# The second adaLN block as TensorE products, the last expert's gate under the second projection ahead of it, its scatter sums in shared banks, query transposes later

## The chip, the cores and the metric

The kernel runs on one core of one Trainium2 chip. The metric is device time in microseconds (us) of one execution, launch to end. The median of three runs before the change is 1257.59 us (1257.53 to 1258.89).

## What is computed

One layer of a latent diffusion backbone, float32, with 256 tokens of width 1024. Cut to what matters here:

```python
sh1, sc1, g1, sh2, sc2, g2 = split(silu(c) @ ada_w + ada_b, 6)      # adaLN: a 1024 x 6144 product with one row
px = modulate(x, norm1_g, sh1, sc1) @ w_in + b_in                    # 5120 columns: q, k, v, hyena, gates
pc = modulate(ctx, norm1_g, sh1c, sc1c) @ w_in + b_in
# rope and qk-norm, differential attention over latent + context keys -> oa
# short convolution and FFT-like long convolution of the hyena columns -> ob
x = x + g1 * ((sigmoid(ga) * (oa @ w_up_a) + sigmoid(gb) * (ob @ w_up_b)) @ w_out)
# top-4-of-32 mixture of experts on modulate(x, norm2_g, sh2, sc2):
#   gate, up = split(h @ w1[e] + b1[e]); y = ((up+1) * gate * sigmoid(1.702 gate)) @ w2[e] + b2[e]
x = x + g2 * moe
```

`ada_w` has six column blocks of 1024. The kernel takes them two at a time: block 0 is sh1 and sc1, block 1 is g1 and sh2, block 2 is sc2 and g2.

## The kernel before

**Two stages.** In the front (from 0 to about 316 us) the adaLN products, the input projection, attention, the hyena branch, the merge and the router are computed. Then 32 experts follow: for each, the tokens chosen (at most 64) are gathered by a product, multiplied by `w1` (eight loads of 1 MB) and by `w2` (four loads of 1 MB), and scattered back by a product.

**What sets the order in the front.** The input projection is cut into pieces (q 0 to 3 and 8 to 11, h1 4 to 7 and 12 to 15, k 16 to 23, v 24 to 31, hv 32 to 39, h0 40 to 47, g0 48 to 55 and so on). The table `TASKS` names for each step of the other work the pieces after which its stages are issued; all engines' queues follow that order. A step `ada` also has its 1-MB load put into SyncE's queue at that place of the load order. All weights pass through 25 slots of 1 MB; the table `ROOM` says how many may hold loads, and `prefetch` issues the next load as soon as one is released, so a load's start is set by the release of an earlier one.

**The second adaLN block before.** `ada_step` (L628) adds up block 1 on VectorE: for each of eight k, two operations on 128x1024 (L639 for the first, L641 for the others) accumulate `col[:, k] * wt` into an SBUF array `AA1`. `ada1` (L981) then adds the 128 partitions up on TensorE: eight products with one column for sh2 (L659, which stand as 16 instructions in the trace) and two of 512 columns for g1 (L985).

**Other steps named below.** `q_out` transposes the rotated queries (`ps_qt`, L850), `k_out` the keys (`ps_kt`, L838, evicted to `KT` at L843 and L844), `v_rows` evicts the values (L974), `hyena` makes the convolved columns `HX` (L879, L880, L882) and `u_rows` transposes them (`ps_u`, L1107), `scores` reduces and exponentiates the attention scores (L1024, L1029). `ada_half` (L652) is the first adaLN block: 8 products per load, in four groups of 32 columns of the array, side by side in one PSUM bank.

**The end.** `up` (L1497) multiplies by `w1` as its loads land, `hidden` makes gate and up on VectorE and ScalarE (L1506 to L1511), `units` transposes the hidden units (L1517, copy L1519), `down` multiplies by `w2` (L1529), `down_last` does so for the last expert (L1586), `out_rows` multiplies by g2 (L1589), `scatter` (L1622) and `scatter_last` (L1593) put the rows back, L1595 adds them to the residual and L1596 writes the output. Under the last five `w1` loads, `last_but_one` scatters expert 30's rows (L1573) and adds them (L1574). Loads run on SyncE's queue (L332), eight outstanding.

## Time and profile before

| | |
|---|---|
| median of three runs | 1257.59 us |
| profiled execution | 1257.4 us |
| its span in the trace | 1255.7 us |
| TensorE busy | 1104.1 us (88%) |
| VectorE busy | 511.1 us (41%) |
| ScalarE busy | 276.7 us (22%) |
| GpSimd busy | 168.6 us (13%) |
| HBM read | 465.07 MB |
| mean granted TensorE clock | 0.982 |

A row of the timeline gives the start, the duration, the engine, the line, the operation with what it writes and reads, and in square brackets how long the engine had been idle before it and which engine, tile and line it was released by. A row of the windows gives for a stretch the busy time and instruction count of each engine, then the granted TensorE clock (1.00 is 2.4 GHz, 0.50 is 1.2 GHz), the share of time in which the DMA engines were busy, and GB/s. SPq is SyncE's queue: such a row is a load's issue, and its duration the time that the queue spent on it, waiting included.

### The profile page before, as it was taken

To read this page: it belongs to the slowest core of one execution; us is meant where nothing else is said; L and a number is where in the kernel's file an instruction comes from. 1 tells how busy PE (TensorE), PEld (TensorE's weight loads), DVE (VectorE), ACT (ScalarE), POOL (GpSimd) and SP (SyncE) were. 2 spreads that over 40 slices of the span, in tenths; PEclk is the share of its full clock that TensorE was granted. 3 is DMA by queue.
4 is the path that set the end of the run, shared out by engine and by line. 5 is a ranking of instruction groups with operands and counts; after the bars stand their busy time and mean duration, and the time that the engine had idled before them with its cause. 6 is when DMAs were issued, how large, how long until landed. Compare 5 with 4: busy or idle time off the path is not lost.

```text
span 1255.7 us, 14038 instructions
## 1 busy us (share of the span) xinstructions
PE 1104.1 (88%) x5547; PEld 532.6 (42%) x5547; DVE 511.1 (41%) x808; ACT 276.7 (22%) x503; POOL 168.6 (13%) x152
## 2 busy tenths in 40 slices
PE   7889789998999899897798879887988797888896
PEld 5678678897433433332242233223322332232222
DVE  5699996967222323331232223123212322223222
ACT  6563464654210111110010011001000100011110
POOL 2386455323000000000000000000000000000000
PEclk9999898999999999999999999999999999999998
DMA  9984534978899999999999999999999999999994
GB/s 335 400 313 148 175 134 191 347 293 358 334 412 417 417 417 417 418 417 418 417 416 417 417 417 417 417 417 417 418 418 418 417 417 418 417 418 417 417 416 177
DMA packets 98450, 467.10 MB, mean 372 GB/s; under 512 B 8800, under 2 KB 9804, under 8 KB 63564
## 3 DMA queue, kind: packets, MB, share of 16 engines
q1 hardware_dynamic: 95056, 462.26, 91.4%
q10 hardware_dynamic: 3324, 3.88, 1.0%
q8 instruction: 46, 0.75, 0.2%
q14 instruction: 24, 0.20, 0.0%
HBM read 465.07 MB, written 1.05 MB: 371 GB/s over the span
## 4 chain that ended last, share of the span: by engine, by line
DMA 54%; PE 28%; DVE 11%; ACT 2%; issue 2%; POOL 1%; ACTq 0%; SPq 0%; DVEq 0%; POOLq 0%
PE ps_eg L1497 6%; PE ps_eu L1497 6%; PE ps_ey L1529 5%; DMA w___w___10__3__4181<-in_exp_w_dram 2%; DMA w____w___18___0__5264<-in_exp_w_dram 2%; DMA w___w___28__7__6440<-in_exp_w_dram 2%; DMA w___w___20__3__5389<-in_exp_w_dram 2%; DMA w___w___11__7__4343<-in_exp_w_dram 2%; DMA w___w___22__3__5666<-in_exp_w_dram 2%; DMA w___w___14__3__4676<-in_exp_w_dram 2%; DMA w___w___24__3__5884<-in_exp_w_dram 2%; DMA w___w___18__3__5171<-in_exp_w_dram 2%; DMA w___w___26__3__6161<-in_exp_w_dram 2%; DMA w___w___27__7__6323<-in_exp_w_dram 2%; DMA w___w___23__7__5828<-in_exp_w_dram 2%
## 5 line engine op out<-in xcount | busy, mean ns | idle before, releaser
L1541 DVE TENSOR_TENSOR yr<-ps_ey,G 64x512 f32<-64x512 f32 x62 | 42.7, 688 | 387.2 <-PE ps_ey L1529 386.6
L479 POOL CAST pick<-both 128x128 fp32r<-128x128 f32 x32 | 24.6, 770 | 842.4 <-PE ps_eu L1380 842.3
L1542 ACT ACTIVATE YS<-yr,wsl 64x512 fp32r<-64x512 f32 x62 | 44.6, 719 | 402.9 <-DVE yr L1541 402.9
L1506 DVE TENSOR_SCALAR ga<-ps_eg 128x512 f32<-128x512 f32 x32 | 22.1, 691 | 163.4 <-PE ps_eg L1497 163.4
L1507 ACT ACTIVATE sg<-ga 128x512 f32<-128x512 f32 x32 | 20.2, 632 | 216.1 <-DVE ga L1506 216.1
L1543 DVE SCALAR_TENSOR_TENSOR YS<-yr,wsl,YS 64x512 fp32r<-64x512 f32 x62 | 46.3, 748 | 48.8 <-ACT YS L1542 48.8
L1452 PE MATMUL ps_xg<-S,XNh 128*128 128x256 f32 x128 | 37.6, 326 | 14.5 <-DVE S L1437 14.5
L1519 ACT COPY at<-ps_at 128x512 f32<-128x512 f32 x32 | 18.8, 586 | 142.6 <-PE ps_at L1517 142.6
L1627 DVE TENSOR_TENSOR X<-X,ps_sc 128x512 f32<-128x512 f32 x60 | 37.4, 680 | 3.0 <-PE ps_sc L1625 3.0
L397 PE MATMUL ps_g<-XTh,wsp 128*128 128x256 f32 x128 | 38.0, 297 | 0.0
L1452 PEld LDWEIGHTS ps_xg<-S,XNh 128*128 128x128 f32 x128 | 28.6, 223 | 19.6 <-DVE S L1437 16.9
L399 PE MATMUL ps_g<-XTh,wsp 128*128 128x256 f32 x128 | 36.5, 285 | 0.0
L398 PE MATMUL ps_g<-XTl,wsp 128*128 128x256 f32 x128 | 36.4, 285 | 0.0
L1452 PE MATMUL ps_xg<-S,XNl 128*128 128x256 f32 x128 | 36.1, 312 | 0.0
L1442 DVE TENSOR_SCALAR RAW<-ps_xg,s,sh 128x256 f32<-128x256 f32 x31 | 16.9, 544 | 35.3 <-ACT RAW L1444 35.3
L1622 PE MATMUL ps_sc<-YS,OT 128*128 128x512 f32 x120 | 30.9, 395 | 0.0
L1444 ACT ACTIVATE RAW<-ps_xg,sh,s 128x256 f32<-128x256 f32 x33 | 18.4, 564 | 49.2 <-PE ps_xg L1452 49.2
L1452 PEld LDWEIGHTS ps_xg<-S,XNl 128*128 128x128 f32 x128 | 28.7, 224 | 0.0
L397 PEld LDWEIGHTS ps_g<-XTh,wsp 128*128 128x128 f32 x128 | 24.6, 192 | 2.3 <-issue 1.8
L1622 PEld LDWEIGHTS ps_sc<-YS,OT 128*128 128x128 f32 x120 | 22.3, 188 | 7.2 <-issue 2.3
L399 PEld LDWEIGHTS ps_g<-XTh,wsp 128*128 128x128 f32 x128 | 24.7, 193 | 0.0
L398 PEld LDWEIGHTS ps_g<-XTl,wsp 128*128 128x128 f32 x128 | 24.6, 192 | 0.1
(1781 smaller groups left out, 2398.8 us busy)
## 6 DMA issues: line engine op xcount, KB each, us to landing
w_x<-in_x_dram SPq DMA_DIRECT2D x2, 512.0 KB, 4.9
w___ada___0__0__88<-in_ada_w_dram SPq DMA_DIRECT2D x2, 512.0 KB, 6.8
w___ada___0__1__91<-in_ada_w_dram SPq DMA_DIRECT2D x2, 512.0 KB, 9.5
w___ada___0__2__95<-in_ada_w_dram SPq DMA_DIRECT2D x2, 512.0 KB, 9.2
w___ada___0__3__98<-in_ada_w_dram SPq DMA_DIRECT2D x2, 512.0 KB, 12.1
...
w___in____h___0__104<-in_w_in_dram SPq DMA_DIRECT2D x1, 1024.0 KB, 12.8
w___ada___1__0__108<-in_ada_w_dram SPq DMA_DIRECT2D x2, 512.0 KB, 12.1
```

The costliest lines, as they stand in the source:

```text
L397: pe.matmul(ps, ahi, bhi, start=start, stop=False, **kw)
L398: pe.matmul(ps, ahi, blo, start=False, stop=False, **kw)
L399: pe.matmul(ps, alo, bhi, start=False, stop=stop, **kw)
L479: gp.tensor_copy(pick.rearrange("p (h c) -> p h c", h=2), src.to_broadcast([P, 2, CAP]))
L1452: pe.matmul(ps[:, kk * T:(kk + 1) * T], xn[:, i, k * P:(k + 1) * P], SS[g][:, i].rearrange("p e c -> p (e c)"), start=(j == 0), stop=(j == 3))
L1497: pe.matmul(ps[64 * h:64 * h + 64, :], XG[e, k], wt[:, b * 1024 + h * 512:b * 1024 + (h + 1) * 512], start=False, stop=(k == KC - 1), skip ...
L1529: pe.matmul(yp[64 * h:64 * h + 64, :], at[:, f % 4, f // 4], wt[:, f % 2, h * 512:(h + 1) * 512], start=(f == 0), stop=(f == KC - 1))
L1541: dve.tensor_tensor(raw, yp[64 * h:64 * h + 64, :], G2[64 * h:64 * h + 64, :], ALU.mult)
L1542: act.activation(hi_[r, cs], raw, AF.Copy, scale=wsl[r, pr:pr + 1])
L1543: dve.scalar_tensor_tensor(lo_[r, cs], raw, wsl[r, pr:pr + 1], hi_.bitcast(F32)[r, cs], ALU.mult, ALU.subtract)
L1622: pe.matmul(ps, OT[pr][:, i], YP[pr][j][:, h * 512:(h + 1) * 512], start=(j == 0), stop=(j == 1 and pr > 0))
L1627: dve.tensor_tensor(xs, xs, ps, ALU.add)
```

## The change

1. `ada_rows_step` takes the place of `ada_step` for block 1: four products per load, `col[:, k]` spread over 32 columns of the array times 512 columns of the weights, into four groups of 32 rows of one held PSUM bank. `AA1` goes, VectorE has no part in it. The steps move from pieces 14, 18, 23, 23, 27, 34, 39, 43 to 29, 30, 32, 34, 36, 38, 40, 42, and their loads with them. `ada1` gets a stage ahead: ScalarE copies the bank to SBUF (`adarows`), four transposes give sh2 and two products g1. `ROOM` follows.
2. The two `q_out` steps move from pieces 22 and 23 to 27, 28 and 28, 29.
3. In the end all eight `w1` loads of expert 31 stand ahead of `w2` of expert 30 (`lead`), `hidden(31)` stands ahead of `down(30)`, and `units(31)` halfway through it. Expert 30's scatter goes into four held banks without VectorE adds, after the first and the third product of the last expert, and the last expert's scatter accumulates into the same banks. The last load is cut in two.

```diff
-    ("later_loads", (), (11,)), ("ctx_norm", (), (13,)), ("ada", (1, 0), (14,)), ("ctx_columns", (), (14, 17)),
...
+    ("later_loads", (), (11,)), ("ctx_norm", (), (13,)), ("ada", (1, 0), (29,)), ("ctx_columns", (), (14, 17)),
...
-    ("ada1", (), (46, 47)), ("u_rows", (), (46, 47)), ("mix", (0, 1), (47, 48, 49)),
+    ("ada1", (), (44, 46, 47)), ("u_rows", (), (46, 47)), ("mix", (0, 1), (47, 48, 49)),
@@ the loads @@
         want(("out", h), [P, 2, 1024], a["w_out"][0, h * 256:(h + 1) * 256].rearrange("(k p) n -> p k n", p=P))
         PIECES += [(("out", h), j) for j in range(4)]
 
+    def lead(e):
+        return KC if e == NE - 1 else LEAD
+
     def want_up(e, ks):
         for k in ks:
             want(("w1", e, k), [P, 2048], a["exp_w1"][0, e, k * P:(k + 1) * P, :])
 
     want_up(0, range(KC))
     for e in range(NE - 1):
-        want_up(e + 1, range(LEAD))
+        want_up(e + 1, range(lead(e + 1)))
         for h in range(4):
             want((("w2", e), h), [P, 2, 1024], a["exp_w2"][0, e, h * 256:(h + 1) * 256].rearrange("(k p) n -> p k n", p=P))
-        want_up(e + 1, range(LEAD, KC))
+        want_up(e + 1, range(lead(e + 1), KC))
 
 
     w2 = a["exp_w2"][0, NE - 1].rearrange("(q f p) n -> p q f n", p=P, q=2)
     for c in range(2):
         for q in range(2):
-            want(("w2", NE - 1, q, c), [P, 4, 512], w2[:, q, :, c * 512:(c + 1) * 512])
+            v = w2[:, q, :, c * 512:(c + 1) * 512]
+            parts_ = [slice(f, 4, 2) for f in range(2)] if q and c else [slice(0, 4)]
+            want(("w2", NE - 1, q, c), [P, 4, 512], [(r, v[:, r]) for r in parts_])
 
     def prefetch():
         while pending and held_by["loads"] < bound[0]:
@@ the second adaLN block @@
 
     ada_ps = {}
 
+
+    ada_n = []
+
+    def ada_rows_step(g, k):
+        wt = w(("ada", g, k))
+        ada_n.append(k)
+        if len(ada_n) == 1:
+            ada_ps[g] = pst(f"ps_ada{g}r", True)
+        for j in range(4):
+            pe.matmul(ada_ps[g][32 * j:32 * j + 32], col[:, k:k + 1].to_broadcast([P, 32]), wt[:, j * 512:(j + 1) * 512],
+                      start=(len(ada_n) == 1), stop=(len(ada_n) == KC))
+        done(("ada", g, k))
+
+
     def ada_step(g, k):
+        if g == 1:
+            return ada_rows_step(g, k)
         wt = w(("ada", g, k))
         if k == 0:
             ada_ps[g] = alloc([P, 2048], f"AA{g}")
...
 
     sh2 = kept([P, 8], "sh2")
     def ada1():
-        c1 = ada_column(1, 1024, "sh2")
+        row = wk.tile([P, 512], F32, tag="sq", name="adarows")
+        act.copy(row, ada_ps[1])
+        unhold("ps_ada1r")
+        yield
+        c1 = pst("ps_sh2", True)
+        for c in range(4):
+            pe.transpose(c1[:, c * P:(c + 1) * P], row[:, c * P:(c + 1) * P], ident)
         g1 = [pst(f"ps_g1{j}", True) for j in range(2)]
         for j in range(2):
-            pe.matmul(g1[j], onesf.to_broadcast([P, P]), ada_ps[1][:, j * 512:(j + 1) * 512], start=True, stop=True)
-        yield
-        dve.tensor_tensor(sh2, c1, bsh2, ALU.add)
+            pe.matmul(g1[j], ident[:, 32 * j:32 * j + 1].to_broadcast([P, P]), row, start=True, stop=True)
+        yield
+        c1 = c1.rearrange("p (c j r) -> p j c r", c=4, j=4)[:, 2:4, :, 0]
+        jc = "p (j c) -> p j c"
+        dve.tensor_tensor(sh2.rearrange(jc, j=2), c1, bsh2.rearrange(jc, j=2), ALU.add)
         unhold("ps_sh2")
         for j in range(2):
             dve.tensor_tensor(G1[:, j * 512:(j + 1) * 512], g1[j], G1[:, j * 512:(j + 1) * 512], ALU.add)
             unhold(f"ps_g1{j}")
-        release("AA1")
 
 
     PTs, ops, es = {}, {}, {}
@@ the end @@
 
     YP, YS = {}, []
 
-    def down(e, at):
-        yp = pst(f"ps_ey{e}")
+    def down(e, at, halfway=None):
+        yp = pst(f"ps_ey{e}", True)
         for f in range(KC):
+            if f == 4 and halfway:
+                halfway()
             wt = w(((("w2", e), f // 2)))
             for h in range(2):
                 pe.matmul(yp[64 * h:64 * h + 64, :], at[:, f % 4, f // 4], wt[:, f % 2, h * 512:(h + 1) * 512],
...
             dve.tensor_tensor(raw, yp[64 * h:64 * h + 64, :], G2[64 * h:64 * h + 64, :], ALU.mult)
             act.activation(hi_[r, cs], raw, AF.Copy, scale=wsl[r, pr:pr + 1])
             dve.scalar_tensor_tensor(lo_[r, cs], raw, wsl[r, pr:pr + 1], hi_.bitcast(F32)[r, cs], ALU.mult, ALU.subtract)
+        unhold(f"ps_ey{e}")
 
     last = {}
 
...
 
     def last_but_one(i, c):
         e, cs = NE - 1, slice(c * 512, (c + 1) * 512)
-        ps = pst(f"ps_sc{e // 2}{i}{c}")
+        ps = last["sum", i, c] = pst(f"ps_last{i}{c}", True)
         for j in range(2):
-            pe.matmul(ps, OT[e // 2][0:64, i], YP[e // 2][j][0:64, cs], start=(j == 0), stop=(j == 1))
-        dve.tensor_tensor(R[0][:, i, cs], R[0][:, i, cs], ps, ALU.add)
+            pe.matmul(ps, OT[e // 2][0:64, i], YP[e // 2][j][0:64, cs], start=(j == 0), stop=False, skip_group_check=True)
 
     between = {(NE - 2, 3): lambda: last_g2(0), (NE - 2, 4): lambda: last_g2(1), (NE - 2, 5): lambda: last_weights(0),
-               (NE - 2, 6): lambda: last_weights(1),
-               **{(NE - 1, 4 + 2 * i + c): lambda i=i, c=c: last_but_one(i, c) for i in range(2) for c in range(2)}}
+               (NE - 2, 6): lambda: last_weights(1)}
 
 
     def down_last(at, q, c):
...
         dve.tensor_tensor(last["Y"][c], last["y", c], last["g2", c], ALU.mult)
 
     def scatter_last(c, i):
-        ps = pst(f"ps_last{i}{c}")
-        pe.matmul(ps, last["wt"][:, i], last["Y"][c], start=True, stop=True)
+        ps = last["sum", i, c]
+        pe.matmul(ps, last["wt"][:, i], last["Y"][c], start=False, stop=True, skip_group_check=True)
         xs = R[0][:, i, c * 512:(c + 1) * 512]
         dve.tensor_tensor(xs, xs, ps, ALU.add)
         (act if i else sp).dma_start(out[0, i * P:(i + 1) * P, c * 512:(c + 1) * 512], xs)
...
     routing_weights()
     act.activation(warm, onesf, AF.Sigmoid)
     up(0, (6, 7))
-    for e in range(NE):
+    for e in range(NE - 1):
         if e:
             up(e, range(LEAD, KC))
         ua = hidden(e)
         if e == 0:
             YS.append(alloc([P, 2, 1024], "YS", F32R))
-        if e < NE - 1:
-            up_bias(e + 1)
+        up_bias(e + 1)
         if e % 2 == 0 and e:
             scatter(e // 2 - 1)
         if e == 1:
             second_bias()
         g = e // 4 + 1
-        if e % 4 == 3 and e < NE - 1:
+        if e % 4 == 3:
             slots_of(g)
             for k2 in range(4):
                 gather(g, k2)
-        elif e < NE - 1:
+        else:
             up(e + 1, range(LEAD - 1))
         at = units(e, ua)
-        if e == NE - 1:
-            break
         if e % 4 == 3:
             weights(g)
             up(e + 1, range(LEAD - 1))
         elif e == 0:
             weights(0)
-        up(e + 1, (LEAD - 1,))
-        down(e, at)
+        up(e + 1, range(LEAD - 1, lead(e + 1)))
+        if e < NE - 2:
+            down(e, at)
+    ua = hidden(NE - 1)
+    units_of = []
+    down(NE - 2, at, lambda: units_of.append(units(NE - 1, ua)))
+    at = units_of[0]
     for c in range(2):
         last["y", c] = pst(f"ps_ey{NE - 1}{c}", True)
     last["Y"] = [wk.tile([P, 512], F32, tag="t1", name=f"Y{c}", bufs=4) for c in range(2)]
     down_last(at, 0, 0)
     down_last(at, 1, 0)
     out_rows(0)
+    last_but_one(0, 0)
+    last_but_one(1, 0)
     down_last(at, 0, 1)
+    last_but_one(0, 1)
+    last_but_one(1, 1)
     scatter_last(0, 0)
-    scatter_last(0, 1)
     down_last(at, 1, 1)
     out_rows(1)
+    scatter_last(0, 1)
     scatter_last(1, 0)
     scatter_last(1, 1)
+    unhold(*[f"ps_last{i}{c}" for i in range(2) for c in range(2)])
     unhold(f"ps_ey{NE - 1}0", f"ps_ey{NE - 1}1")
     for key in list(W):
         done(key)

...
```

TensorE's row, before, at the place where the second adaLN block is finished (`ps_sh` is sh2, `ps_g` is g1, `ps_u` the hyena rows):

```order
L399 MATMUL ps_h_1323<-XTh,wsp_1374 128x256
L659 MATMUL ps_sh_1489<-onesf,AA_689 128x1 x8
L985 MATMUL ps_g_1498<-AA_689,onesf 128x512
L985 MATMUL ps_g_1499<-AA_689,onesf 128x512
L1107 MATMUL ps_u_1503<-ident,HX 128x128 x4
```

And after the change:

```order
L403 MATMUL ps_h_1333<-XTh,wsp_1390 128x256
L1008 MATMUL ps_sh_1509<-ident,adarows 128x128 x4
L1011 MATMUL ps_g_1514<-adarows,ident 128x512
L1011 MATMUL ps_g_1515<-adarows,ident 128x512
L1134 MATMUL ps_u_1519<-ident,HX 128x128 x4
```

The place in the row stays; what it reads comes from ScalarE (`adarows`) where it came from VectorE (`AA`).

ScalarE's row after the change at that place (`PAIR` is the exponentials of the scores, `pthv` and `HX` the hyena step, `wsp` the split weights of g0):

```order
L1056 ACTIVATE PAIR,ss_1355<-ps_s_1356,ss_1355,B_130 128x512
L1056 ACTIVATE PAIR,ss_1355<-ps_s_1357,ss_1355,B_130 128x512
L893 ACTIVATE pthv_1441<-ps_hv_1132,B_130 128x256
L897 ACTIVATE HX<-pthv_1441,B_130 128x256
L893 ACTIVATE pthv_1444<-ps_hv_1132,B_130 128x256
L897 ACTIVATE HX<-pthv_1444,B_130 128x256
L371 CAST wsp_1447<-w___in____g___0__1152 128x512 x2
L1003 COPY adarows<-ps_ada1r 128x512
```

The copy stands at the end of that row of work, behind the two exponentials.

VectorE's row before, at the hyena columns that TensorE's `ps_u` reads (`ss` is what the exponentials wait for):

```order
L641 SCALAR_TENSOR_TENSOR AA_689<-w___ada___1__6__832,col,AA_689 128x1024 x2
L879 SCALAR_TENSOR_TENSOR HX<-pthv_1348,B_130,HX 128x255
L880 SCALAR_TENSOR_TENSOR HX<-pthv_1348,B_130,HX 128x255
L882 TENSOR_TENSOR HX<-HX 128x256
L879 SCALAR_TENSOR_TENSOR HX<-pthv_1351,B_130,HX 128x255
L880 SCALAR_TENSOR_TENSOR HX<-pthv_1351,B_130,HX 128x255
L882 TENSOR_TENSOR HX<-HX 128x256
L1024 TENSOR_REDUCE ss_1339<-ps_s_1340 128x1
L1024 TENSOR_REDUCE ss_1339<-ps_s_1341 128x1
L1026 TENSOR_SCALAR ss_1339<-ss_1339,B_130 128x1 x2
L641 SCALAR_TENSOR_TENSOR AA_689<-w___ada___1__7__941,col,AA_689 128x1024 x2
```

And after:

```order
L899 SCALAR_TENSOR_TENSOR HX<-pthv_1364,B_130,HX 128x255
L900 SCALAR_TENSOR_TENSOR HX<-pthv_1364,B_130,HX 128x255
L902 TENSOR_TENSOR HX<-HX 128x256
L899 SCALAR_TENSOR_TENSOR HX<-pthv_1367,B_130,HX 128x255
L900 SCALAR_TENSOR_TENSOR HX<-pthv_1367,B_130,HX 128x255
L902 TENSOR_TENSOR HX<-HX 128x256
L1051 TENSOR_REDUCE ss_1355<-ps_s_1356 128x1
L1051 TENSOR_REDUCE ss_1355<-ps_s_1357 128x1
L1053 TENSOR_SCALAR ss_1355<-ss_1355,B_130 128x1 x2
```

The two adaLN operations ahead of the chain and the two behind it are gone; the rest of the row is the same.

TensorE's row at the end, before, from the last gate's transposes on (`ps_at` is the transposed hidden units, `ps_ey` the last expert's output, `ps_last` its scatter):

```order
L1517 MATMUL ps_at_7002<-ident,ua_6996 128x128 x4
L1586 MATMUL ps_ey_7009<-w___w___31__0__0__6824,at_7007 64x512 x4
L1586 MATMUL ps_ey_7009<-w___w___31__1__0__6830,at_7007 64x512 x4
L1586 MATMUL ps_ey_7010<-w___w___31__0__1__6836,at_7007 64x512 x4
L1593 MATMUL ps_last_7026<-Y_7011,WT_6880 128x512
L1593 MATMUL ps_last_7030<-Y_7011,WT_6880 128x512
L1586 MATMUL ps_ey_7010<-w___w___31__1__1__6850,at_7007 64x512 x4
L1593 MATMUL ps_last_7039<-Y_7012,WT_6880 128x512
L1593 MATMUL ps_last_7043<-Y_7012,WT_6880 128x512
```

And after, from the same transposes on:

```order
L1544 MATMUL ps_at_6985<-ident,ua_6970 128x128 x4
L1558 MATMUL ps_ey_6976<-w____w___30___2__6825,at_6942 64x512 x4
L1558 MATMUL ps_ey_6976<-w____w___30___3__6832,at_6942 64x512 x4
L1614 MATMUL ps_ey_7008<-w___w___31__0__0__6838,at_6990 64x512 x4
L1614 MATMUL ps_ey_7008<-w___w___31__1__0__6844,at_6990 64x512 x4
L1603 MATMUL ps_last_7021<-YS,OT_6588 128x512 x2
L1603 MATMUL ps_last_7024<-YS,OT_6588 128x512 x2
L1614 MATMUL ps_ey_7009<-w___w___31__0__1__6850,at_6990 64x512 x4
L1603 MATMUL ps_last_7031<-YS,OT_6588 128x512 x2
L1603 MATMUL ps_last_7034<-YS,OT_6588 128x512 x2
L1621 MATMUL ps_last_7021<-Y_7010,WT_6895 128x512
L1614 MATMUL ps_ey_7009<-w___w___31__1__1__6864,at_6990 64x512 x4
```

Three scatter products of the last expert follow. The last expert's transposes stand under the second projection of the one before, and expert 30's four scatters (L1573 before, between the last `w1` products) stand between the last expert's own products.

## Rows read from the trace of the kernel before

**Rows 1.** The page's GB/s in 40 equal slices of the span.
```profile
GB/s 335 400 313 148 175 134 191 347 293 358 334 412 417 417 417 417 418 417 418 417 416 417 417 417 417 417 417 417 418 418 418 417 417 418 417 418 417 417 416 177
```

**Rows 2.** Windows: busy us of each engine by stretch, clock, DMA share, GB/s.
```profile
100.00:160.00 60.00, 51.78 (x309) 46.15 (x308) 56.30 (x67) 22.99 (x47) 34.09 (x23) 0.90 0.48 163
```

**Rows 3.** Timeline of TensorE: its waits between 88 and 163 us.
```profile
92.02 0.63 PE L850 MATMUL ps_qt<-ident,t1q 128*128 128x128 f32 x4 [3.83 <-DVE t1q L829]
...
127.88 1.26 PE L838 MATMUL ps_kt<-ident,t1k 128*128 128x128 f32 x8 [1.47 <-DVE t1k L831]
132.76 0.45 PE L838 MATMUL ps_kt<-ident,t1k 128*128 128x128 f32 x1 [3.62 <-DVE KT L844]
...
155.22 3.58 PE L659 MATMUL ps_sh<-onesf,AA 128*128 128x1 f32 x16 [3.12 <-DVE AA L641]
158.66 3.37 PE L985 MATMUL ps_g<-AA,onesf 128*128 128x512 f32 x4
162.90 0.66 PE L1107 MATMUL ps_u<-ident,HX 128*128 128x128 f32 x4 [0.42 <-ACT PAIR L1029]
```

**Rows 4.** Windows behind two of these waits.
```profile
92.00:98.00 6.00, 5.98 (x22) 4.86 (x23) 5.89 (x10) 1.51 (x3) 0.22 (x1) 0.72 0.42 165
132.00:138.00 6.00, 5.24 (x26) 5.27 (x27) 4.93 (x10) 3.88 (x10) 1.51 (x2) 0.53 0.97 342
```

**Rows 5.** Windows of L641 alone: VectorE's busy time, clock, DMA share, GB/s.
```profile
60.00:160.00 100.00, 20.03 (x14) 0.92 0.60 212
```

**Rows 6.** Timeline of TensorE: steps of the first adaLN block, and what precedes.
```profile
43.08 0.28 PE L399 MATMUL ps_h<-XTh,wsp 128*128 128x256 f32 x1
43.29 1.07 PE L652 MATMUL ps_ada<-w___ada___1__0__108,cT 128*32 128x256 f32 x16
...
44.18 1.05 PE L652 MATMUL ps_ada<-w___ada___1__1__111,cT 128*32 128x256 f32 x16
```

**Rows 7.** Timelines of VectorE and ScalarE around the hyena columns and the scores.
```profile
148.82 2.51 DVE L882 TENSOR_TENSOR HX<-HX 128x256 f32<-128x256 f32 x1
...
156.39 0.42 DVE L882 TENSOR_TENSOR HX<-HX 128x256 f32<-128x256 f32 x1
...
152.69 0.78 ACT L1029 ACTIVATE PAIR<-ps_s,ss,B 128x512 f32<-128x512 f32 x1 [7.63 <-DVE ss L1026]
...
156.22 1.12 ACT L367 CAST wsp<-w___in____g___0__1038 128x512 fp32r<-128x512 f32 x2
```

**Rows 8.** The chain that ended last: its final steps (start, us, what).
```profile
1231.55 0.69 DVE X L1574
...
1235.11 1.10 PE ps_at L1517 x4
...
1236.92 6.94 PE ps_ey L1586 x24
1243.87 1.91 PE ps_last L1593 x4
1245.78 1.89 PE ps_ey L1586 x8
...
1250.46 0.69 DVE X L1595
```

**Rows 9.** DMA issues, 1205 to 1256 us: KB each, us from issue to landing.
```profile
w___w___31__0__0__6824<-in_exp_w_dram SPq DMA_DIRECT2D x1, 1024.0 KB, 20.1
w___w___31__0__1__6836<-in_exp_w_dram SPq DMA_DIRECT2D x1, 1024.0 KB, 20.2
w___w___31__1__1__6850<-in_exp_w_dram SPq DMA_DIRECT2D x1, 1024.0 KB, 13.5
```

**Rows 10.** Timeline of SyncE's queue: when these were issued.
```profile
1211.31 0.38 SPq L332 DMA_DIRECT2D w___w___31__0__0__6824<-in_exp_w_dram  x1
...
1216.39 9.24 SPq L332 DMA_DIRECT2D w___w___31__0__1__6836<-in_exp_w_dram  x1
1225.72 2.38 SPq L332 DMA_DIRECT2D w___w___31__1__1__6850<-in_exp_w_dram  x1
```

More of the change, by code (lines that the diff above doesn't have):

```diff
@@ L37 @@
     ("filter_decay", (1,), (2,)), ("dft_parts", (0,), (2,)), ("filter_decay", (0,), (6,)), ("ctx_stats", (), (8,)),
-    ("later_loads", (), (11,)), ("ctx_norm", (), (13,)), ("ada", (1, 0), (14,)), ("ctx_columns", (), (14, 17)),
+    ("later_loads", (), (11,)), ("ctx_norm", (), (13,)), ("ada", (1, 0), (29,)), ("ctx_columns", (), (14, 17)),
     ("ctx_modulate", (0,), (15,)), ("ctx_modulate", (1,), (15,)), ("q_raw", (0,), (16, 18, 19)), ("ctx_modulate", (2,), (16,)),
     ("q_raw", (1,), (16, 19, 20)), ("tables", (), (16,)), ("vec2_cols", (), (17, 17)), ("hyena", (3, "h1", 4), (18, 20)),
-    ("ada", (1, 1), (18,)), ("ctx_modulate", (3,), (18,)), ("q_rope", (0,), (19,)), ("hyena", (2, "h1", 4), (19, 22)),
@@ L42 @@
-    ("hyena", (1, "h1", 4), (21, 22)), ("q_rope", (1,), (21,)), ("q_out", (0,), (22, 23)), ("q_out", (1,), (22, 23)),
-    ("hyena", (0, "h1", 4), (22, 23)), ("ada", (1, 4), (23,)), ("ada", (1, 3), (23,)), ("k_raw", (0,), (25, 26, 27)),
-    ("k_raw", (1,), (26, 28, 29)), ("ada", (1, 2), (27,)), ("k_raw", (3,), (27, 28, 30)), ("k_raw", (2,), (28, 29, 30)),
+    ("ada", (1, 1), (30,)), ("ctx_modulate", (3,), (18,)), ("q_rope", (0,), (19,)), ("hyena", (2, "h1", 4), (19, 22)),
+    ("hyena", (1, "h1", 4), (21, 22)), ("q_rope", (1,), (21,)), ("q_out", (0,), (27, 28)), ("q_out", (1,), (28, 29)),
@@ L45 @@
+    ("hyena", (0, "h1", 4), (22, 23)), ("ada", (1, 4), (32,)), ("ada", (1, 3), (34,)), ("k_raw", (0,), (25, 26, 27)),
+    ("k_raw", (1,), (26, 28, 29)), ("ada", (1, 2), (36,)), ("k_raw", (3,), (27, 28, 30)), ("k_raw", (2,), (28, 29, 30)),
     ("k_stats", (), (30,)), ("k_rope", (1,), (30,)), ("lambda_", (), (30,)), ("k_rope", (2,), (32,)), ("k_rope", (3,), (32,)),
-    ("k_rope", (0,), (33,)), ("v_rows", (1,), (33,)), ("k_out", (3,), (34, 35)), ("ada", (1, 5), (34,)),
+    ("k_rope", (0,), (33,)), ("v_rows", (1,), (33,)), ("k_out", (3,), (34, 35)), ("ada", (1, 5), (38,)),
@@ L47 @@
     ("v_rows", (2,), (35,)), ("release", ("BIN",), (35,)), ("v_rows", (3,), (36,)), ("k_out", (0,), (36, 37)),
-    ("k_out", (2,), (36, 39)), ("k_out", (1,), (36, 37)), ("v_rows", (0,), (37,)), ("ada", (1, 6), (39,)),
+    ("k_out", (2,), (36, 39)), ("k_out", (1,), (36, 37)), ("v_rows", (0,), (37,)), ("ada", (1, 6), (40,)),
     ("scores", (0, 0), (40, 42, 43)), ("hyena", (1, "hv", 8), (40, 41)),
     ("hyena", (0, "hv", 8), (40, 41)), ("scores", (0, 1), (43, 45, 46)), ("dft_parts", (1,), (43,)),
-    ("hyena", (2, "hv", 8), (43, 44)), ("ada", (1, 7), (43,)), ("hyena", (3, "hv", 8), (43, 44)), ("mix", (0, 0), (44, 45, 46)),
@@ L52 @@
-    ("ada1", (), (46, 47)), ("u_rows", (), (46, 47)), ("mix", (0, 1), (47, 48, 49)),
+    ("hyena", (2, "hv", 8), (43, 44)), ("ada", (1, 7), (42,)), ("hyena", (3, "hv", 8), (43, 44)), ("mix", (0, 0), (44, 45, 46)),
+    ("ada1", (), (44, 46, 47)), ("u_rows", (), (46, 47)), ("mix", (0, 1), (47, 48, 49)),
     ("scores", (1, 0), (47, 48, 49)), ("pt_out", (0, 0), (48, 50)),
```

9 rows, old and new, of the table ROOM are left out of this document.

## The prediction, made before the changed kernel ran

> **What bounds the kernel now.** I read the slices of the span first. From the eleventh slice, about 320 us, to the last but one the DMA engines move 412 to 418 GB/s in nearly every slice; ahead of that it is 134 to 400, and in the last slice 177 [rows 1]. So three parts. The middle is bound by its loads and no edit here touches their number. The front is not bound by loads: the windows give 163 GB/s between 100 and 160 us, where VectorE is busy 56.30 of 60 us [rows 2]. The last slice waits for a chain. What the front saves moves the whole stream of loads forward, 1 to 1, since the stream starts when the first expert's products release slots; what the end saves adds to it.
>
> In the front I asked the timeline of TensorE for its waits. Up to 160 us there are five, and VectorE ends nearly all: 3.83 us for the rotated queries, 1.47 and 3.62 for the keys, 3.12 for the adaLN sums, 0.42 ahead of the hyena rows [rows 3]. Each long wait is paid twice: the granted clock behind it is 0.72 and 0.53 in windows of 6 us [rows 4], of which 1.00 is the upper level, 2.4 GHz, and 0.50 the lower, 1.2 GHz. The loss, 6 x 0.28 = 1.7 us and 6 x 0.47 = 2.8 us, is time TensorE had work.
>
> The end is read from the chain that ended last: a VectorE add at 1231.55, the last gate, transposes at 1235.11, 24 products from 1236.92, a scatter, 8 products, a scatter, and the last add at 1250.46 [rows 8]. Of the last four loads the first was issued at 1211.31 and took 20.1 us, so it landed at 1231.4; the last was issued at 1225.72, took 13.5 and landed at 1239.2 [rows 9, 10]. TensorE first reads the former 5.5 us after it landed.
>
> **The change, part by part.** *Query transposes.* They move five pieces later, where the rotated queries are long done; the wait of 3.83 and its clock loss of 1.7 go. The transposes themselves (the four in the row last 0.63, so about 1.2 us for both steps [rows 3]) go from there too and come back five pieces on. At the first v piece TensorE stands 3.8 + 1.7 + 1.2 = 6.7 us earlier.
>
> *Block 1 off VectorE.* L641 takes 20.03 us of VectorE between 60 and 160 us in 14 operations [rows 5]; with the two of L639 sixteen go. VectorE is full there, so its rows for keys, values and hyena columns come forward by as much as TensorE allows.
>
> *Block 1 on TensorE.* A step is four products of 512 columns in four groups. The nearest row is a step of the first block: eight products of 256 columns in the same four groups, as many columns in all. One starts at 43.29, the next at 44.18: 0.89, and the row is 1.07 long [rows 6]. I take 0.87 a step. That assumes that the groups run side by side here as there; if they ran one after the other, four times that, 3.5 us. Entering this mode shows nearly nothing: the first step starts 0.21 us behind the last product ahead of it, whose like follow each other at 0.12 [rows 6]. I allow 0.09 us for each change of mode, two a step. The Trainium skill, "TensorEngine Tiling (Array Packing)", section Key Properties, says that changing the tiling mode drains TensorE. By that rule sixteen such changes would each cost the rest of a product in flight, at 0.28 each 4.5 us; the trace agrees at most with the 0.09 of this one place.
>
> *From the k pieces to the h0 pieces.* Five steps lie ahead of piece 37: 5 x 0.87 = 4.4, and 0.9 for ten changes of mode; with the query transposes (1.2) 6.5 is given back, so TensorE is level again, 0.2 us ahead. The key waits, 1.47 + 3.62 and 2.8 of clock, are 7.9; two short evictions between VectorE and ScalarE stay, so I count 7.0 of it. A sixth step costs 1.0. At the end of the hv pieces: 0.2 + 7.0 - 1.0 = 6.2 us earlier. Here one bank less is free (the sums hold it from piece 29 to 44), so TensorE runs less far ahead of its evictions: this may give back 0 to 4 us (a key wait's size), and I take nothing, since the evictions are earlier too.
>
> *The adaLN sums.* Before: TensorE stops at 155.22 - 3.12 = 152.10, and reaches `ps_u` at 162.90, so wait, sixteen one-column products (3.4 between starts), two sums for g1 (3.37) and the last wait take 10.8 [rows 3]. After: it arrives 6.2 earlier but with two more steps behind it (2.0): 147.9. What it reads now comes from ScalarE, whose copy stands behind two exponentials, which wait for VectorE's hyena columns [rows 7]. That chain starts when the hv products end, 6.2 earlier, hence the exponentials at 146.5 instead of 152.69. From there to the cast that ends at 157.3 it took 4.7 us; the copy comes at 151.2 and takes about 0.6. TensorE waits from 147.9 to 151.8, and the clock falls behind it as behind the others. Four transposes at the lower clock take 1.1 for a row of the same shape [rows 8], the two g1 products 3.37 [rows 3]: `ps_u` at 156.3, against 162.90. Gain of the front 6.6. What follows hangs from TensorE and shifts with it.
>
> The loads: eight move later in the queue, the k and v loads ahead of them come earlier. DMA engines are busy 48% between 100 and 160 us [rows 2], and TensorE waited for none of its loads there, so nothing is priced; an order that made one late would cost at most a load's wait, some us, and I keep that for the top of the range.
>
> *The end.* The order after shows the last expert's transposes ahead of the second half of expert 30's `w2`. All loads keep their places in time, so TensorE is through with expert 30 when its last block has landed (that was the last `w1` block's place), about 1231. The gate, transposes and copy from 1231.55 to 1236.92 leave the path, 5.4 us. It starts on the first `w2` block at 1231.4: to 1233.3 with the 1.9 us of eight products [rows 8], the second block by 1235.8 (its load lands about 1234.0, midway between those beside it in the queue), expert 30's scatters 1.3, the third 1.9, to 1239.0 (its load was issued at 1216.39 and took 20.2, so landed at 1236.6), scatters to 1240.3, one of the last expert's, then the last eight products to 1243.2, Y (0.7), scatters to 1245.9. Against 1250.46 it is 4.5 earlier. The four VectorE adds of L1574 go, of which only the last was on the path. That the clock stays up with the wait gone is in the 1.9; at the lower clock it would be 3.5 for the first eight, 1.6 less gained. Bounds 2.5 and 6.
>
> **Sum.** Against the profiled execution, 1257.4 (span 1255.7 and 1.7 around it, 0.2 below the median): 6.6 + 4.5 = 11.1, so 1246.3; I say **1246**.
>
> **Rivals.** *The wait at the sums goes too.* The hyena operations last 2.51 us where GpSimd works and 0.42 for the same shape where it does not [rows 7]. If with 20 us less of VectorE's rows these meet less, the chain to the exponentials shortens by 4 us, the copy is there first and neither the wait nor the slow clock comes. Then `ps_u` stands at about 147.9 + 0.7 + 1.7 = 150.3, a front gain of 12.6: 1240. The Trainium skill, "SBUF — State Buffer", section Who interferes with whom, says that VectorE reading two inputs and GpSimd reading SBUF block each other for a whole instruction; fewer such rows is what would give this. Against it: the hyena operations and GpSimd's splits are all still there.
>
> *The front gives nearly nothing.* The next VectorE or ScalarE chain (rows of the scores, keys by one bank less) ends at its old time: the front gains 0 to 2, and 1257.4 - 1 - 4.5 = 1252. For it: VectorE at 94% is not idle after losing 20 of 100 us. Against: what is queued on it hangs from TensorE's pieces.
>
> *The groups run one after the other.* Then a step is 3.5, eight cost 21 more on TensorE, which is the front's path: 1246 + 21 = 1267, slower. It decides from 0.87 + 11/8 = 2.2 us per step on. Against it: sixteen instructions of 256 columns within 1.07 us are 0.07 each, a quarter of the 0.28 that as many columns take over the whole array in the same rows [rows 6]. For it: the broadcast column is a new operand.
>
> *It does not do what it says:* a late load or the held bank in the front costs as much as the end gives, 4 to 5 us: 1257, no change.
>
> **How the numbers follow.** Forecast (1243 to 1250) 0.54; both waits go, 1240, 0.16; front eaten, 1252, 0.17; no change 0.06; slower 0.07. Range 1238 to 1253 leaves out the last two and a little of the tails of the others, some 0.2. A measurement here can tell about 0.2%, 2.5 us: faster 0.87, same 0.06, slower 0.07.
>
> **What would show it.** In the changed kernel: no wait at the query transposes and the clock at 1.0 in that window; `ps_ada1r` steps of 0.9 us; a wait of 3 to 4 us for ScalarE ahead of `ps_sh`, with `ps_u` near 156; the stream of loads at its full rate 6 to 7 us earlier; no pause of TensorE between the last `w1` product and the last load, and the last add about 4.5 us closer to the last load's landing. A wait for a load in the front, steps of 3 us, or keys still waiting by 3 us would break it.

## The result and the profile after the change

The changed kernel takes 1244.58 us (median of four runs, 1242.98 to 1248.44), the kernel before 1258.24 beside it. The ratio is 0.9893, 95% interval 0.9876 to 0.9911: faster by 11 to 16 us. The profiled execution took 1245.22, its span is 1243.5. The same kernel, run again later beside two others (e9 below), had a median of 1242.01 and a ratio of 0.9857 (0.9828 to 0.9886). One of its four executions took 1399.13 us at a mean clock of 0.746, where the others have 0.98 to 0.99; it and two like it (1288.61 in e5, 1277.95 of the kernel before beside e9) are left out of the ratios.

Where it went is read from three places. The first is TensorE's timeline between 85 and 185 us. In the kernel before it held the waits of [rows 3]; here there is none until 155 us:

```profile
103.96 0.60 PE L870 MATMUL ps_qt<-ident,t1q 128*128 128x128 f32 x4
...
110.17 0.39 PE L403 MATMUL ps_v<-wsp,CTl 128*128 128x512 f32 x1
110.48 1.06 PE L645 MATMUL ps_ada1r<-w___ada___1__0__490,col 128*32 128x512 f32 x8
111.48 0.50 PE L401 MATMUL ps_v<-wsp,XTh 128*128 128x512 f32 x1
111.81 0.39 PE L402 MATMUL ps_v<-wsp,XTh 128*128 128x512 f32 x1
...
150.57 0.60 PE L1008 MATMUL ps_sh<-ident,adarows 128*128 128x128 f32 x4
151.01 1.88 PE L1011 MATMUL ps_g<-adarows,ident 128*128 128x512 f32 x4
152.73 0.60 PE L1134 MATMUL ps_u<-ident,HX 128*128 128x128 f32 x4
155.51 0.66 PE L1134 MATMUL ps_u<-ident,HX 128*128 128x128 f32 x4 [2.19 <-ACT PAIR L1056]
180.06 0.66 PE L1074 MATMUL ps_p<-ident,PAIR 128*128 128x128 f32 x4 [3.88 <-DVE PAIR L1066]
```

The query transposes, the adaLN steps, the sums and the first hyena transposes follow without a bracket. The windows say the same. Of the changed kernel (busy us of each engine with its instruction count, then clock, DMA share, GB/s):

```profile
60.00:150.00 90.00, 90.00 (x550) 72.50 (x549) 65.19 (x98) 49.61 (x97) 56.93 (x52) 1.00 0.69 251
92.00:98.00 6.00, 6.00 (x28) 4.99 (x27) 5.89 (x7) 1.33 (x3) 4.48 (x4) 1.00 0.01 1
132.00:138.00 6.00, 6.00 (x51) 4.75 (x53) 2.40 (x6) 3.65 (x9) 2.48 (x2) 1.00 1.05 381
```

And of the kernel before in the longest of these stretches:

```profile
60.00:150.00 90.00, 81.07 (x462) 70.86 (x461) 83.54 (x103) 41.77 (x81) 59.58 (x49) 0.94 0.66 235
```

TensorE is busy 90.00 of 90 us at the upper clock; before it was 81.07 at a mean of 0.94. VectorE's 83.54 us of work there have become 65.19. The two short windows are those of [rows 4], where the clock was 0.72 and 0.53.

The second place is the end, the chain that ended last in the changed kernel (start, us, what):

```profile
1206.71 19.51 DMA w___w___31__1__0__6844<-in_exp_w_dram
...
1226.27 1.94 PE ps_ey L1614 x8
1228.20 1.14 PE ps_last L1603 x4
1229.34 1.87 PE ps_ey L1614 x8
1231.21 1.14 PE ps_last L1603 x4
1232.34 1.06 PE ps_last L1621 x2
1233.40 1.87 PE ps_ey L1614 x8
1235.27 2.79 PE ps_last L1621 x6
...
1238.08 0.69 DVE X L1623
```

In [rows 8] a gate, transposes and a copy lay between the last loads and the last products. Here the chain goes from a load's landing straight into products.

The third place gives the sizes. One execution and the next differ in their first 50 us by up to 6 us, in code that the change doesn't touch. So I measure two stretches: from the second adaLN transposes (`ps_adac`, near 50 us) to the first expert's first product (`ps_eg`), and from there to the last add. In the kernel before these two rows of TensorE's timeline are

```profile
48.23 0.44 PE L671 MATMUL ps_adac<-ident,adarow 128*128 128x128 f32 x2 [1.28 <-DVE adarow L667]
...
315.56 1.08 PE L1497 MATMUL ps_eg<-w___w___0__0__2244,RAW 128*64 128x512 f32 x4
```

and in the changed kernel

```profile
50.99 0.44 PE L691 MATMUL ps_adac<-ident,adarow 128*128 128x128 f32 x2 [0.56 <-DVE adarow L687]
...
308.36 1.08 PE L1524 MATMUL ps_eg<-w___w___0__0__2258,RAW 128*64 128x512 f32 x4
```

So the front stretch is 315.56 - 48.23 = 267.3 before and 257.4 after: 10 us gained. The rest, to the last add at 1250.46 and 1238.08, is 934.9 and 929.7: 5.2 us gained. The changed kernel's profiled execution began 2.8 us late, which is why its span is only 12.2 shorter. The same two rows in all the runs, in us:

| run | front stretch | from there to the last add |
|---|---|---|
| before | 267.3 | 934.9 |
| changed | 257.4 | 929.7 |
| e1 the end alone | 266.4 | 929.8 |
| e2 the front alone | 255.8 | 935.2 |
| e3 query transposes alone | 266.2 | 934.7 |
| e4 adaLN alone | 264.8 | 934.8 |
| e5 one group | 271.4 | 930.9 |
| e6 VectorE's work back | 280.7 | 930.8 |
| e7 two waits given room | 257.1 | 930.2 |
| e8 last load whole | 257.1 | 931.1 |
| e9 changed, again | 256.1 | 930.5 |
| e10 inverse at 58 | 255.6 | 931.0 |
| e11 inverse at 57 | 251.5 | 930.2 |
| e12 the same, again | 252.4 | 929.9 |

Each row is one execution. Where two runs have the same code in a stretch they still differ: by 0.9 us in the unchanged front (before and e1), by up to 1.6 in the changed one (changed, e2, e8, e9) and by up to 1.3 in the second column under the changed end. Differences of that size say nothing.

### The profile page after: what moved, and what is told of

Its sections match the earlier page's. It is cut to its first block, busy times and chain, and to the rows that moved or that the text cites. A ratio compares the mean times of both kernels' runs of the same rounds, so it can differ in the third digit from the quotient of the medians.

```text
span 1243.5 us, 14125 instructions
## 1 busy us (share of the span) xinstructions
PE 1110.0 (89%) x5599; PEld 534.6 (43%) x5599; DVE 482.6 (39%) x788; ACT 277.9 (22%) x504; POOL 161.6 (13%) x152
## 3 DMA queue, kind: packets, MB, share of 16 engines
q10 hardware_dynamic: 3324, 3.88, 1.1%
HBM read 465.07 MB, written 1.05 MB: 375 GB/s over the span
## 4 chain that ended last, share of the span: by engine, by line
PE 46%; DMA 40%; DVE 9%; ACT 2%; issue 2%; POOL 1%; ACTq 0%; SPq 0%; DVEq 0%; POOLq 0%
PE ps_eg L1524 9%; PE ps_eu L1524 9%; PE ps_ey L1558 7%; PE ps_xg L1479 4%; DMA w___w___9__7__4139<-in_exp_w_dram 2%; DMA w___w___27__7__6337<-in_exp_w_dram 2%; DMA w____w___18___0__5278<-in_exp_w_dram 2%; DMA w___w___26__3__6175<-in_exp_w_dram 2%; DMA w___w___10__3__4195<-in_exp_w_dram 2%; DMA w___w___18__3__5185<-in_exp_w_dram 2%; DMA w___w___22__3__5680<-in_exp_w_dram 2%; DMA w___w___14__3__4690<-in_exp_w_dram 2%; DMA w___w___11__7__4357<-in_exp_w_dram 2%; DMA w___w___13__7__4634<-in_exp_w_dram 2%; DMA w___w___25__7__6119<-in_exp_w_dram 2%; DMA w___w___21__7__5624<-in_exp_w_dram 2%
## 5 line engine op out<-in xcount | busy, mean ns | idle before, releaser
L1479 PE MATMUL ps_xg<-S,XNh 128*128 128x256 f32 x128 | 41.9, 351 | 14.4 <-DVE S L1464 14.4
L1479 PE MATMUL ps_xg<-S,XNl 128*128 128x256 f32 x128 | 40.2, 336 | 0.0
L1479 PEld LDWEIGHTS ps_xg<-S,XNh 128*128 128x128 f32 x128 | 31.7, 248 | 19.6 <-DVE S L1464 17.0
L1479 PEld LDWEIGHTS ps_xg<-S,XNl 128*128 128x128 f32 x128 | 31.8, 248 | 0.0
## 6 DMA issues: line engine op xcount, KB each, us to landing
w___ada___0__2__95<-in_ada_w_dram SPq DMA_DIRECT2D x2, 512.0 KB, 10.6
w___in____h___0__104<-in_w_in_dram SPq DMA_DIRECT2D x1, 1024.0 KB, 12.2
```

Of the source, the lines that this page charges most:

```text
L1479: pe.matmul(ps[:, kk * T:(kk + 1) * T], xn[:, i, k * P:(k + 1) * P], SS[g][:, i].rearrange("p e c -> p (e c)"), start=(j == 0), stop=(j == 3))
```

## The experiments

**e1 and e2: which half gives what.** e1 is the kernel before with the part of the diff under "the end" and its loads; e2 is the kernel before with the tables and the second adaLN block.

```diff
+    down(NE - 2, at, lambda: units_of.append(units(NE - 1, ua)))
...
+    last_but_one(0, 0)
+    last_but_one(1, 0)
```

```diff
     def ada_step(g, k):
+        if g == 1:
+            return ada_rows_step(g, k)
```

> The kernel before with part 3 alone (the end). If the end's saving is its own: the last add stands 4.5 to 5.5 us closer to the last load's landing, 1252.5 to 1253.5 against 1258. If the end was hidden behind the last loads and the whole gain came from the front: 1257 to 1258.

> The kernel before with parts 1 and 2 alone (adaLN block 1 on TensorE, query transposes later). If the front's saving passes on 1 to 1: 7 to 10 us, 1248 to 1251. If the stream of loads does not start earlier: 1257 to 1258.

e1: 1252.89 us, ratio 0.9960 (0.9947 to 0.9974). e2: 1249.05, ratio 0.9936 (0.9919 to 0.9953). The kernel before beside both had 1257.65. The savings by medians are 4.8 and 8.6, together 13.4, against 13.7 for the whole change. Each passes through, neither hides behind the loads, and the table shows each in its own stretch alone.

**e3 and e4: are the two edits in the front separate?**

e3, on the kernel before:

```diff
-("q_out", (0,), (22, 23)), ("q_out", (1,), (22, 23))
+("q_out", (0,), (27, 28)), ("q_out", (1,), (28, 29))
```

e4, on e2:

```diff
-("q_out", (0,), (27, 28)), ("q_out", (1,), (28, 29))
+("q_out", (0,), (22, 23)), ("q_out", (1,), (22, 23))
```

> The kernel before with the query transposes moved and nothing else. If VectorE's rows are the bound and not the place of the transposes, the key waits grow by about what the query wait was: gain 0 to 2 us, 1256 to 1258. If each wait can be taken away by itself: 3.8 us and 1.7 of clock, 1252.5.

> Parts 1 and 2 without the move of the query transposes: adaLN block 1 on TensorE alone. If VectorE's rows are the bound, its 6 us ahead of the query transposes go too, that wait of 3.8 us shrinks to under 1, and the gain is nearly the whole of the front's, 6 to 9 us: 1249 to 1252. If the transposes' place was what made TensorE wait, the wait stays at 3 to 4 us and the gain is 2 to 4: 1254 to 1256.

e3: 1258.63 us, ratio 1.0009 (0.9992 to 1.0025): nothing. Its waits of TensorE:

```profile
108.50 0.66 PE L850 MATMUL ps_qt<-ident,t1q 128*128 128x128 f32 x4 [3.04 <-DVE RAW L799]
...
130.41 0.39 PE L397 MATMUL ps_hv<-XTh,wsp 128*128 128x256 f32 x1 [1.78 <-ACT wsp L367]
132.09 0.39 PE L399 MATMUL ps_hv<-XTh,wsp 128*128 128x256 f32 x1 [1.17 <-POOL wsp L375]
138.35 1.08 PE L838 MATMUL ps_kt<-ident,t1k 128*128 128x128 f32 x4 [3.93 <-DVE KT L844]
```

The wait of 3.83 at 92 us [rows 3] is gone and 3.04, 1.78 and 1.17 stand where there were none. TensorE's waits between 60 and 170 us add up to 12.8 us here and to 12.5 in the kernel before. VectorE's row is as long as before, so a wait that is taken away comes back a little later.

e4: 1252.95 us, ratio 0.9963 (0.9949 to 0.9976), 4.7 of e2's 8.6. Here my expectation fell. The wait on the query transposes stays:

```profile
91.55 1.08 PE L865 MATMUL ps_qt<-ident,t1q 128*128 128x128 f32 x4 [3.60 <-DVE t1q L844]
```

though VectorE has 6 us less to do ahead of it. Its timeline in e4 tells why:

```profile
65.59 0.69 DVE L536 COPY CT<-ps_c 128x512 f32<-128x512 f32 x1 [3.61 <-PE ps_c L531]
...
77.07 1.38 DVE L735 TENSOR_SCALAR CT<-CT,mods 128x256 f32<-128x256 f32 x2 [2.24 <-ACT CTh L734]
...
80.17 2.94 DVE L842 TENSOR_TENSOR swq<-RAW,HX 128x256 f32<-128x256 f32 x2
```

Where the adaLN operations stood VectorE now waits, 3.61 us for TensorE and 2.24 for ScalarE, as long as the operations took, and the rotation that took 0.74 us in the kernel before takes 2.94, while GpSimd works on its splits of 128x512 (in the kernel before it was at operations of 128x32 then). The freed time ahead of the transposes bought nothing there. So neither edit does it alone: e3's 1.1 us of the front stretch are no more than the spread of that stretch, e4 gains 1.6 to 2.5 by its trace (4.7 by the medians), the two together (e2) 10.6 to 11.5 by the trace and 8.6 by the medians.

**e5: are the four groups what makes a step cheap?**

```diff
-            pe.matmul(ada_ps[g][32 * j:32 * j + 32], col[:, k:k + 1].to_broadcast([P, 32]), wt[:, j * 512:(j + 1) * 512],
+            r = 32 * j if len(ada_n) == 1 else 0
+            pe.matmul(ada_ps[g][r:r + 32], col[:, k:k + 1].to_broadcast([P, 32]), wt[:, j * 512:(j + 1) * 512],
...
```

> The changed kernel, but seven of the eight adaLN steps put their four products into one group of 32 columns of the array, so that none runs beside another; sh2 and g1 come out wrong by that. If the groups side by side are what makes a step cost 1.0 us: a step's row 3 to 4 us, seven steps 14 to 21 us more on TensorE, of which VectorE's waits hide little: 1257 to 1264. If a step costs as much in one group: 1244 to 1246.

1258.0 us, ratio 0.9997 (0.9984 to 1.0009). By the instructions of the line in e5 (count, min/median/max ns, first and last start):

```profile
L646 PE MATMUL ps_ada1r<-w___ada___1__0__490,col x8: 592/604/617, 108.1 to 108.6; 128*32 128x512 f32 x8
L646 PE MATMUL ps_ada1r<-w___ada___1__1__500,col x8: 592/592/617, 112.0 to 115.0; 128*32 128x512 f32 x8
```

The first step spreads over the groups: eight starts within 0.5 us, 1.1 in all. The second has one group: starts over 3.0 us, 3.6 in all. Seven such steps are 2.5 x 7 = 17.5 us more; the front stretch grew 14.1. A wait of 2.2 at the hyena rows went; the 1.2 that is left is within the spread of the stretch. The groups side by side are worth all that the change gained, the end's gain included: without them the kernel is back at the time before.

**e6: is it VectorE's time?**

```diff
+        for h in range(2):
+            hs = slice(h * 1024, (h + 1) * 1024)
+            dve.scalar_tensor_tensor(wt[:, hs], wt[:, hs], col[:, k:k + 1], wt[:, hs], ALU.mult, ALU.add)
         done(("ada", g, k))
```

> The changed kernel with VectorE's work given back and no more: behind each adaLN step's products VectorE does two operations of 128x1024 on the weights just used, whose result nobody reads. If the front's saving comes from VectorE's free time: its waits come back, 3 to 8 us lost, 1248 to 1252. If it comes from the sums' way over ScalarE and from the order alone: 1244 to 1246.

1268.65 us, ratio 1.0069 (1.0047 to 1.0091): 24 us lost against the changed kernel, the front stretch 23 longer. The direction is the theory's, the size is three times what I wrote. Five of its waits of TensorE:

```profile
129.65 0.39 PE L401 MATMUL ps_hv<-XTh,wsp 128*128 128x256 f32 x1 [2.58 <-ACT wsp L371]
136.45 1.12 PE L861 MATMUL ps_kt<-ident,t1k 128*128 128x128 f32 x4 [2.06 <-DVE V L997]
140.73 1.94 PE L861 MATMUL ps_kt<-ident,t1k 128*128 128x128 f32 x8 [3.16 <-DVE KT L867]
153.83 0.96 PE L1050 MATMUL ps_s<-KT,QT 64*128 64x512 f32 x6 [1.76 <-DVE KT L867]
169.31 0.68 PE L1011 MATMUL ps_sh<-ident,adarows 128*128 128x128 f32 x4 [3.42 <-ACT adarows L1006]
```

The operations stand at pieces 29 to 42 here, where VectorE's row for keys and values is densest, and not from piece 14 on as in the kernel before. There the time lost is as long as their some 24 us. Two things go with it. The operations rewrite the weights that a step's products read, so VectorE also waits for those products (3.81 us ahead of the first pair of operations, at 110.57), and the slots come free later; but no engine waited for a load between 60 and 200 us. And the 24 us are over twice what the front had gained: e6 shows that VectorE's time at this place is on the path, not how much of the gain it is.

**e7, e10, e11 and e12: the waits that are left.** e7 gives room to the two last rows of the first fence above; e10 and e11 also to what came late then.

```diff
-("u_rows", (), (46, 47))                 ("pt_out", (1, 0), (54, 57))
+("u_rows", (), (47, 48))                 ("pt_out", (1, 0), (56, 57))
-("inverse", (), (55, 57, 58, 60, 60))
+("inverse", (), (58, 60, 61, 62, 62))    # e10
+("inverse", (), (57, 59, 60, 61, 61))    # e11 and e12; e7 leaves this row as it was
```

> The changed kernel with two of TensorE's remaining waits given room: the transposes of the hyena rows one piece later (pieces 47, 48), those of the third score block two pieces later (piece 56). If a wait of 2.2 and one of 3.9 us with 3.4 us of slower clock behind it are TensorE's own time on the path: 4 to 9 us faster, 1236 to 1241. If VectorE or ScalarE ends the next wait at the old time: 1243 to 1246.

e7: 1244.2 us, ratio 0.9874 (0.9848 to 0.9900), the front stretch 257.1: nothing. Both waits went (2.19 to 0.78, 3.88 to none), and one new wait took it all:

```profile
185.04 0.58 PE L401 MATMUL ps_y<-FG,Y 128*128 128x256 f32 x1 [4.71 <-ACT Y L1172]
```

> The kernel of the run with the two waits given room, and the products that come next late (the inverse transform's, which waited 4.7 us there for ScalarE) three pieces later too. If that was the last of the chain: TensorE has no wait over 1.5 us between 150 and 200 us and its clock stays up, 6 to 9 us faster, 1236 to 1239. If work further on (keys of the second half, the gathered hyena rows) ends at its old time: 1241 to 1245.

> The same with those products two pieces later. If the wait of 4.7 us shrinks by the pieces that now stand ahead (two of some 1.5 us each, two key products beside): a wait of 1 to 2 us is left, 1237 to 1241. If the next wait takes its place: 1241 to 1245.

> The kernel of the run before this (hyena rows one piece later, third score block's transposes and inverse transform's products two pieces later) timed in more rounds. If the 5 us that its trace shows between the first 50 us and the first expert's products are its own and not that execution's: 1237 to 1240, a ratio of 0.982 to 0.986 to the kernel before. If they were that execution's: 1241 to 1244.

e10: 1242.78 us, ratio 0.9870 (0.9844 to 0.9896), no better than e9. Between 150 and 200 us it has no wait over 0.8, but at 209 us

```profile
208.99 1.97 PE L1074 MATMUL ps_p<-ident,PAIR 128*128 128x128 f32 x8 [4.25 <-DVE PAIR L1066]
```

takes it back. e11, one piece earlier, has a smaller one in that place:

```profile
206.62 1.38 PE L1074 MATMUL ps_p<-ident,PAIR 128*128 128x128 f32 x8 [1.75 <-DVE PAIR L1066]
```

It took 1238.94 us, ratio 0.9841 (0.9815 to 0.9866), and again in e12 1237.81, ratio 0.9848 (0.9824 to 0.9872). By medians that is 3 to 7 us under the changed kernel's two (1242.01 and 1244.58), and its front stretch, 251.5 and 252.4, is 4 to 6 us under 256.1 and 257.4. It is the fastest of all here. In all three VectorE does two steps of the third adaLN block (L659 and L661) ahead of these scores. In e11 and e12 they start at 196.70 and 196.56, in e10 at 199.08, and behind the longer wait the granted clock is 0.52 from 209 to 215 us, where e11 has 1.00 and e12 0.81. Whether that block could go to TensorE like the second is not tested. The intervals of the ratios overlap with the changed kernel's (e9 0.9828 to 0.9886), so its lead in time rests on the medians of both pairs and on the traces.

**e8 and e9.** e8 joins the last load again (`parts_ = [slice(0, 4)]`); e9 is the changed kernel once more.

> The changed kernel with the last load in one transfer. In the trace of the changed kernel TensorE comes to the last block 4 us after it landed: no change, within 0.2%. If the split brought its landing forward where TensorE waits: 1 us slower.

> The changed kernel as it is, beside the next two on the same chip: 1242 to 1246.

e8: 1242.58 us, ratio 0.9865 (0.9843 to 0.9886); no difference can be told, as the trace had it: in the changed kernel TensorE starts on the last block at 1233.33, and the two halves, issued from 1217.78 on, take 11.7 us at the median.

## Why the prediction was right, step by step

The forecast was 1246, the time 1244.58 and 1242.01 in its two sets. It holds, but one step of the front and the size of the end were off, both to the cautious side: the later set lies 1 us under the forecast's own band of 1243 to 1250. How near the number came is in part luck, as step 5 shows. The times below have the 2.8 us of late start taken off.

1. *The query wait goes; 6.7 us earlier at the first v piece.* Before that piece began at 96.83; after at 93.07 - 2.8 = 90.3, so 6.5. Right. The clock in the window is 1.00. By e3, though, this gain would have come back later as other waits; it is kept because VectorE's row is shorter behind it.
2. *A step costs 0.87, and 0.18 for two changes of mode.* Nearly right. From the last product ahead of a step (110.17) to the second behind it (111.81) are 1.64 us; without a step two spacings of 0.23 would lie there, so a step costs 1.18, not 1.05, 1.0 us more in eight. e5 shows the price without the groups, a row of 3.6. The Trainium skill, "TensorEngine Tiling (Array Packing)", section Key Properties, has each change of mode drain TensorE; by the forecast's estimate of 0.28 a change a step would be 1.4. The trace's 1.18 leaves 0.31 for the two changes beside the 0.87, more than the 0.18 allowed and about half of that estimate.
3. *The key waits go but for 0.9; 6.2 us earlier at the end of the hv pieces.* They go entirely. The last hv product began at 139.58 before and at 136.04 - 2.8 = 133.2 after: 6.3. The 0.9 of waits that went beyond the forecast and the 0.8 that six steps cost beyond it cancel. No wait shows that the bank less cost anything.
4. *TensorE comes to the sums at 147.9.* It came at 150.57 - 2.8 = 147.8. Right.
5. *It waits there until 151.8 for ScalarE's copy, and the clock falls.* Wrong, and this is the step that failed. The copy was done 1.8 us ahead:

```profile
143.63 0.78 ACT L1056 ACTIVATE PAIR<-ps_s,ss,B 128x512 f32<-128x512 f32 x1 [1.11 <-DVE ss L1053]
...
148.21 0.57 ACT L1003 COPY adarows<-ps_ada1r 128x512 f32<-128x512 f32 x1
```

   I had moved the chain of the hyena columns as a block, with its old durations. In the kernel before it took from 142.13 to 151.25, when the scores' reduction starts:

```profile
142.13 1.05 DVE L879 SCALAR_TENSOR_TENSOR HX<-pthv,B,HX 128x255 f32<-128x255 f32 x1 [0.37 <-ACT HX L877]
...
151.25 1.28 DVE L1024 TENSOR_REDUCE ss<-ps_s 128x1 f32<-128x512 f32 x2
```

   In the changed kernel VectorE's timeline reads

```profile
138.59 1.33 DVE L899 SCALAR_TENSOR_TENSOR HX<-pthv,B,HX 128x255 f32<-128x255 f32 x1 [3.31 <-ACT HX L897]
139.96 0.48 DVE L900 SCALAR_TENSOR_TENSOR HX<-pthv,B,HX 128x255 f32<-128x255 f32 x1
140.48 0.42 DVE L902 TENSOR_TENSOR HX<-HX 128x256 f32<-128x256 f32 x1
...
142.19 1.28 DVE L1051 TENSOR_REDUCE ss<-ps_s 128x1 f32<-128x512 f32 x2
```

   It takes 3.6 us in place of 9.1. GpSimd is what differs. It is idle from 139.65 to 142.08:

```profile
137.11 2.54 POOL L379 TENSOR_TENSOR wsp<-w___in____h___1__1107,wsp 128x512 fp32r<-128x512 f32 x2 [1.89 <-ACT wsp L371]
142.08 2.58 POOL L379 TENSOR_TENSOR wsp<-w___in____h___1__1107,wsp 128x512 fp32r<-128x512 f32 x2 [2.43 <-ACT wsp L371]
```

   where in the kernel before it worked through that chain:

```profile
140.64 3.70 POOL L375 TENSOR_TENSOR wsp<-w___in____h___1__1021,wsp 128x512 fp32r<-128x512 f32 x2 [1.32 <-ACT wsp L367]
144.61 2.71 POOL L375 TENSOR_TENSOR wsp<-w___in____h___1__1021,wsp 128x512 fp32r<-128x512 f32 x2 [0.27 <-ACT wsp L367]
147.39 1.11 POOL L422 CAST FG<-GB 128x1024 fp32r<-128x1024 f32 x1
148.59 2.46 POOL L423 TENSOR_TENSOR FG<-GB,FG 128x1024 fp32r<-128x1024 f32 x1
```

   Each of the operations shrinks from between 1.05 and 2.51 us to 0.42 or 0.48, but for the first, which still meets the split that ends at 139.65. No run was made for this alone, but all fourteen traces bear it out: between 60 and 170 us the chain's last operation (`HX<-HX`, 128x256) takes 0.42 or 0.43 us in the 37 rows where it stands beside GpSimd's work for under 0.4 us, and 1.14 to 2.51 in the 17 where it does for over 1 us. This was the first rival's mechanism, with a chance of 0.16 (the rival had the chain shorter by 4 us; it is 5.5), and the trace agrees with the Trainium skill, "SBUF — State Buffer", section Who interferes with whom, which has a VectorE operation with two inputs from SBUF and a GpSimd operation that reads SBUF shut each other out. But the rival's 12.6 was not reached either: one row further the second half of the hyena transposes waits 2.19 us for the exponentials. 12.6 - 2.2 = 10.4 lies in what was measured (9.9 to 11.5 in the changed kernel, e2 and e9). That wait, which neither the forecast nor the rival names, brought the time back from the rival's 1240 towards 1246; that part is luck.
6. *All that follows shifts with it.* Right: the wait of 3.9 at the third score block stayed in its place and size, and e7, e10 and e11 show what it and its successors were holding back.
7. *The end gains 4.5.* It gained 5.2, in e1 5.1. The order of steps was the forecast's. TensorE goes from the landing of the second block into products without a pause, as the chain above shows, at a clock of 1.00 (1226 to 1238 us), where it was 0.50 from 1236 to 1240 in the kernel before. Of what it gained more, 0.4 is the second block, whose products start 917.9 us behind the first expert's (1226.27 - 308.36) where the forecast has 918.3 (1235.8 less their own 1.9, less 315.56); 0.2 is in the steps from there to the last add. The sign "no pause" between the last `w1` product and the last load did not come as it stands: TensorE waits 0.5 to 0.9 us for each of most blocks there, since the loads still set the pace.
8. *Rivals.* The front that gives nothing is refuted by e2, the serial groups by the rows and by e5. e5 also confirms how the serial price was worked out: forecast 2.6 us more a step, measured 2.5. One argument against the serial groups does not hold as it stands: 0.07 us an instruction is a spacing, 0.28 is the duration of a row whose like start 0.12 apart, so their ratio is not a quarter of anything; what shows the groups side by side is e5.
